# A small store of zeros as ScalarE's first DMA, ahead of the first tile's store, in a channel shuffle

## Chip, cores and metric

The kernel runs on one core of a Trainium2 chip. The metric is device time in microseconds (us), the median of several executions. All timed executions compared here ran in the fast state, at a granted clock of 1.0; runs looked at once have no state of their own ("unknown"), but the same clock. Traces are of one execution each, with times counted from the start of that execution's span.

## The reference

The input is float32, 16 x 64 x 64 x 256. The 256 channels are regarded as 8 groups of 32 and transposed inside each row:

```
x = x.reshape(batch, h, w, groups, channels_per_group)
x = x.transpose(0, 1, 2, 4, 3)
x = x.reshape(batch, h, w, c)
```

There is no arithmetic. 67.11 MB are read and 67.11 MB are written.

## The kernel before

The rows are cut into 22 tiles of 128 partitions. `_SIZES` gives the rows per partition: a 24-row tile moves 128 rows of 24 KB, 3 MB. SyncE loads a tile, VectorE shuffles it in pieces of 8 rows into PSUM, ScalarE copies each piece back to the same buffer, and ScalarE issues the store. So loads and stores go through different queues: in the trace, q1 is SyncE's (loads) and q10 is ScalarE's (stores). There are eight tile buffers, and loads run far ahead. SyncE, VectorE and ScalarE are engines of the core; PSUM is the buffer in which the shuffled pieces stand. A packet is one DMA record of the trace: one row of a tile is one packet, 24 KB for most tiles.

```
_SIZES = [24] * 20 + [8, 24]
_BUFS = 8
_PIECE = 8
# ... set-up cut ...
first = 0
for q in _SIZES:
    buf = pool.tile([P, biggest * c], F32, name="buf")
    nc.sync.dma_start(out=buf[:, : q * c], in_=rows(x_flat, first, q))
    for k in range(0, q, _PIECE):
        piece = buf[:, k * c : (k + _PIECE) * c]
        bounce = psum.tile([P, _PIECE * c], F32, name="bounce")
        nc.vector.tensor_copy(
            out=bounce.rearrange("p (i j g) -> p i j g", j=CPG, g=G),
            in_=piece.rearrange("p (i g j) -> p i j g", g=G, j=CPG),
        )
        nc.scalar.copy(out=piece, in_=bounce)
    nc.scalar.dma_start(out=rows(out_flat, first, q), in_=buf[:, : q * c])
    first += P * q
```

Of the kernel before, what the change touches and what calls it, by code (L numbers as in the profile page):

```python
# [1 line left out]

# [4 lines left out]


F32 = mybir.dt.float32
P = 128  # L10

_SIZES = [24] * 20 + [8, 24]
_BUFS = 8

_PIECE = 8


@with_exitstack
def kernel(
    ctx: ExitStack,  # L20
    tc: tile.TileContext,
    x: bass.AP,
    groups: bass.AP,
    out: bass.AP,
):
    nc = tc.nc
    b, h, w, c = x.shape
    G = int(groups)
    CPG = c // G
    assert G * CPG == c  # L30
    assert sum(_SIZES) * P == b * h * w
    biggest = max(_SIZES)

    x_flat = x.rearrange("b h w c -> (b h w c)")
    out_flat = out.rearrange("b h w c -> (b h w c)")

    pool = ctx.enter_context(tc.tile_pool(name="pool", bufs=_BUFS))
    psum = ctx.enter_context(
        tc.tile_pool(name="psum", bufs=2, space=bass.MemoryType.PSUM)
    )  # L40

    def rows(flat, first, q):

        return flat[first * c : (first + P * q) * c].rearrange("(p f) -> p f", p=P)

    ctx.enter_context(tc.manual_schedule(engines=None))
    first = 0
    for q in _SIZES:
        buf = pool.tile([P, biggest * c], F32, name="buf")
        nc.sync.dma_start(out=buf[:, : q * c], in_=rows(x_flat, first, q))  # L50
        for k in range(0, q, _PIECE):
# [11 lines that stand above are left out]
# [1 line left out]
_INS = ['x', 'groups']  # L64
_OUTS = [((16, 64, 64, 256), 'float32')]

_NUMBERS = {'groups': 8}


# [26 lines left out]
```

## Time and profile before

| what | value |
|---|---|
| time, median of 3 before the prediction | 317.67 us (317.38 to 317.92) |
| span of the profiled execution | 315.9 us |
| bytes moved | 134.24 MB, mean 425 GB/s |
| VectorE busy, ScalarE busy | 72%, 38% |

The page of the kernel before, cut to the rows on which the reading rests. The span is cut into 40 equal slices of 7.9 us; a DMA digit is the busy share in tenths, and GB/s is what the 16 DMA engines moved in that slice.

```profile
span 315.9 us, 289 instructions
...
DVE 227.9 (72%) x64; ACT 120.3 (38%) x65; POOL 0.2 (0%) x4
...
DMA  8999999999999999999999999999999999999997
GB/s 296 439 442 380 436 429 433 433 439 433 423 442 433 426 442 426 426 442 426 433 436 427 433 436 436 433 426 437 433 423 448 423 429 444 429 423 433 439 432 302
```

The DMA engines are busy everywhere; no other engine is. Three slices fall short: the first (the start), the last (the end) and the fourth, with 380 GB/s. The fourth covers 23.7 to 31.6 us. The timeline of ScalarE shows what happens there: ScalarE issues its very first DMA, the store of the first tile. The columns are start, duration, engine, line, operation, and in brackets what the engine waited for.

```profile
11.10 1.28 ACT L58 ACT_TABLE_LOAD   x1 [11.10 <-DMA buf<-in_x_dram]
...
23.68 0.37 ACTq L59 DMA_DIRECT2D out_dram<-buf  x1
...
164.29 0.34 ACTq L59 DMA_DIRECT2D out_dram<-buf  x1
```

The last line is a later store.

To size this, I spread each DMA packet's bytes evenly over the packet's recorded duration, and call "loss" the length of a window less the bytes moved in it divided by 433 GB/s. The figure 433 is the most that any window of 5 us moved in this trace; it also is what 16 packets of 24 KB in every 0.908 us come to, the spacing measured in undisturbed traffic. The trace stays at 432 to 433 GB/s in nearly every 5 us window (53 of 63), so an undisturbed one has a "loss" of 0.00 to 0.01 us. All losses below are such sums over one trace. (The recorded texts took theirs at a slightly higher rate, which no trace shows and which is cut there; their losses are greater by about 0.02 us for each 5 us of a window. For the experiments I converted the sums from that rate, so the last digit can be off by one.)

```
kernel before, window     loss     seen in the packets
  0 to  5 us              2.84 us  first load packet at 1.74 us; first packets take 1.3 to 2.3 us
  5 to 25 us              0.02 us  loads alone, 0.912 us a packet of 24 KB
 25 to 30 us              0.75 us  load packets stretch to 1.2 to 1.9 us; first store packet at 27.69 us
164 to 174 us             0.02 us  stores begin again after a pause of 9.5 us
```

The windows view prints the same dip (columns: window, its length, busy time of VectorE, ScalarE and GpSimd with instruction counts, TensorE clock, DMA share, GB/s). It books all of a packet's bytes at the packet's start, so short windows jump by some per cent; the loss sums do not.

```profile
15.00:25.00 10.00, 10.00 (x3) 5.28 (x3) 0.00 (x0) 1.00 1.00 433
25.00:35.00 10.00, 10.00 (x4) 5.60 (x3) 0.00 (x0) 1.00 1.01 401
35.00:45.00 10.00, 10.00 (x4) 5.59 (x3) 0.00 (x0) 1.00 1.00 433
...
154.00:164.00 10.00, 0.00 (x0) 0.00 (x0) 0.00 (x0) 1.00 1.01 433
164.00:174.00 10.00, 7.38 (x3) 5.50 (x3) 0.00 (x0) 1.00 1.01 433
```

The last two lines are the restart of stores at 164 us, where 0.02 us is lost.

### The profile page before, as it was taken

The numbers are of one execution on the slowest core, as the hardware profiler recorded it, in microseconds if no ns is written. First come the engines' busy times: TensorE is split into PE (matmuls) and PEld (weight loads), VectorE is DVE, ScalarE is ACT, GpSimd is POOL, SyncE is SP. The second block draws the span as 40 slices with busy tenths as digits, with TensorE's granted clock in tenths as the row PEclk, the third lists the DMA queues.
The fourth block names the chain that finished last, engine by engine and source line by source line (L and its number), as shares of the span: only waits on it lengthen the run. The fifth ranks groups of instructions, "written<-read, shape, count | busy, mean of one in ns | idle before, by whom it ended". The sixth has DMA issues, their size and how long they took to land.

```text
span 315.9 us, 289 instructions
## 1 busy us (share of the span) xinstructions
DVE 227.9 (72%) x64; ACT 120.3 (38%) x65; POOL 0.2 (0%) x4
## 2 busy tenths in 40 slices
DVE  0699999959587685957008986999970299999900
ACT  0354455525252424330015416545500444555420
POOL 0000000000000000000000000000000000000000
DMA  8999999999999999999999999999999999999997
GB/s 296 439 442 380 436 429 433 433 439 433 423 442 433 426 442 426 426 442 426 433 436 427 433 436 436 433 426 437 433 423 448 423 429 444 429 423 433 439 432 302
DMA packets 6338, 134.24 MB, mean 425 GB/s; under 512 B 704, under 2 KB 704, under 8 KB 704
## 3 DMA queue, kind: packets, MB, share of 16 engines
q1 hardware_dynamic: 3168, 67.11, 49.9%
q10 hardware_dynamic: 3168, 67.11, 49.4%
q14 instruction: 2, 0.02, 0.0%
HBM read 67.11 MB, written 67.11 MB: 425 GB/s over the span
## 4 chain that ended last, share of the span: by engine, by line
DVE 54%; another core or an unknown queue 23%; issue 8%; ACT 5%; DMA 3%; DVEq 1%; ACTq 0%
DVE bounce L54 54%; ACT buf L58 5%; DMA buf<-in_x_dram 3%; DVEq L91 1%; ACTq L59 0%; DVEq L54 0%; ACTq L58 0%
## 5 line engine op out<-in xcount | busy, mean ns | idle before, releaser
L54 DVE COPY bounce<-buf 128x2048 f32<-128x2048 f32 x64 | 227.9, 3636 | 72.6 <-ACT buf L58 38.8
L58 ACT COPY buf<-bounce 128x2048 f32<-128x2048 f32 x64 | 119.0, 1866 | 171.1 <-DVE bounce L54 115.3
L58 ACT ACT_TABLE_LOAD x1 | 1.3, 1283 | 11.1 <-DMA buf<-in_x_dram 11.1
L77 POOL MEMSET const-bfloat16-1.0<- 128x1 bf16 x1 | 0.1, 102 | 0.0
L77 POOL MEMSET const-uint8-127<- 128x1 uint8 x1 | 0.1, 101 | 0.0
L77 POOL MEMSET const-float32-0.0<- 128x1 f32 x1 | 0.1, 99 | 0.2 <-issue 0.2
L77 POOL MEMSET const-float32-1.0<- 128x1 f32 x1 | 0.1, 98 | 0.0
## 6 DMA issues: line engine op xcount, KB each, us to landing
buf<-in_x_dram SPq DMA_DIRECT2D x21, 3072.0 KB, 58.4
out_dram<-buf ACTq DMA_DIRECT2D x21, 3072.0 KB, 24.2
buf<-in_x_dram SPq DMA_DIRECT2D x1, 1024.0 KB, 46.0
out_dram<-buf ACTq DMA_DIRECT2D x1, 1024.0 KB, 15.8
```

Source lines behind the costliest of these rows:

```text
L54: nc.vector.tensor_copy(out=bounce.rearrange("p (i j g) -> p i j g", j=CPG, g=G), in_=piece.rearrange("p (i g j) -> p i j g", g=G, j=CPG),)
L58: nc.scalar.copy(out=piece, in_=bounce)
L77: nc = _bacc.Bacc("TRN2", target_bir_lowering=False, num_devices=1)
L91: with _tile.TileContext(nc) as tc:
```

## The change

The intent: whatever the first store costs, pay it at the start, where ScalarE and VectorE are idle (until about 11 us) and the loads are slow anyway (296 GB/s in the first slice). A tile of zeros is made, and 512 B of each of the first tile's 128 rows is stored as ScalarE's first DMA. The first tile's real store waits for it and overwrites it, so the result is right.

```diff
+_EARLY = 128
 ...
+    early = ctx.enter_context(tc.tile_pool(name="early", bufs=1))
 ...
+    if _EARLY:
+        zeros = early.tile([P, _EARLY], F32, name="zeros")
+        nc.vector.memset(zeros, 0.0)
+        nc.scalar.dma_start(out=rows(out_flat, 0, _SIZES[0])[:, :_EARLY], in_=zeros)
```

More of the change, by code (lines that the diff above doesn't have):

```diff
@@ L46 @@
     ctx.enter_context(tc.manual_schedule(engines=None))
+    if _EARLY:
+        zeros = early.tile([P, _EARLY], F32, name="zeros")
+        nc.vector.memset(zeros, 0.0)
+        nc.scalar.dma_start(out=rows(out_flat, 0, _SIZES[0])[:, :_EARLY], in_=zeros)
     first = 0
-    for q in _SIZES:
+    for t, q in enumerate(_SIZES):
         buf = pool.tile([P, biggest * c], F32, name="buf")
```

## The prediction

> What bounds the kernel now: the 16 DMA engines. The page's slice row shows DMA at 9 tenths in every slice but the first and last, 134.24 MB at a mean of 425 GB/s over a 315.9 us span; VectorE is busy 72%, ScalarE 38%. [...] its packet records give 432 to 433 GB/s in nearly every 5 us window, for loads, stores or both. So time falls only where the DMA engines lose it. [...] 0 to 5 us loses 2.85 us (the first load packet starts at 1.74 us, and the first packets take 1.5 to 2.3 us against 0.912 us later); 25 to 30 us loses 0.77 us; the end about 2 us; all else 0.03 us per 5 us.
>
> The loss at 25 to 30 us is what the change aims at. ScalarE issues its first store at 23.68 us; from 25.2 us the running load packets stretch from 0.91 to 1.2 to 1.9 us, and the first store packet starts only at 27.69 us. The page shows 380 GB/s in the fourth slice. It is the first use of that queue, not the mixing of loads and stores: at 164.29 us a store is issued to an empty store queue amid full load traffic, its first packet comes 3.5 us later, and the rate stays at 432 GB/s. So a first-use cost of about 0.75 us, once.
>
> What the change adds. A VectorE memset, when VectorE idles until 11.05 us: free. One ScalarE issue (0.34 to 0.37 us in the timeline) near 1 us, where ScalarE idles until 11.10 us: free. 64 KB in 128 rows of 512 B: from the trace's 8 KB packets (0.309 us) and 24 KB packets (0.912 us) I estimate 0.03 us per row, 8 per engine, about 0.2 us of DMA time. The first tile's store waits for this store too, which should land before 8 us: no wait. The extra DMA turns the eight completion semaphores by one: SyncE's sixth load now waits for the first to land (about 11 us), where before the seventh was the first that waited. Five loads of about 7.2 us each are queued, so nothing starves. The later waits (stores held by a load's semaphore, as at 138 to 164 us) keep their pattern.
>
> How much is critical. The engines are full from 30 to 310 us, so what is saved at 27 us moves everything after it. Uncertain is where the first-use cost goes when paid at 1 to 5 us: hidden in the loads' own slow start (gain 0.55 to 0.75 us), or added to it (net loss 0.2 us). Hiding, at least in part, seems likelier.
>
> Predicted time: 317.3 us against 317.67; range 316.6 to 318.1. Faster by over 2%: 0.01; within 2%: 0.98; slower by over 2%: 0.01.
>
> What would show it. Right: the fourth slice rises from 380 to about 430 GB/s; the first tile's store gets its first packet about 3.5 us after issue, with no stretched load packets; the first slice's 296 GB/s falls by no more than 10. Wrong: the fourth slice stays low (the cost is then the first large store's), or the first slice loses what the fourth gains.
>
> What would make it wrong: those two, or the semaphore turn changing when stores are held, so that the last stores, whose issue follows VectorE's chain (last issue 302.46 us, first packet 306.56 us), no longer queue behind one another.

The sum: 317.67 us less 0.55 to 0.75 us if the first-use cost hides in the loads' slow start (316.92 to 317.12), or plus 0.2 us if it is added to it (317.87); the 317.3 lies between, nearer to the first. At 433 GB/s the losses that it lists come to 2.84 us (0 to 5 us), 0.75 us (25 to 30 us), about 1.9 us (the end) and 0.01 us for each other 5 us.

## The result and the profile after

| | median | range | runs |
|---|---|---|---|
| before | 317.63 us | 317.38 to 317.92 | 6 |
| after | 317.83 us | 317.73 to 318.17 | 6 |

The ratio is 1.0007, with a 95% interval of 0.9995 to 1.002: the same time. A ratio here is the mean time of one kernel's fast runs over that of the other's fast runs of the same rounds, so it is not quite the ratio of the medians.

The page of the kernel after, the same rows and the early store's own line (size, and us from issue to landing):

```profile
span 316.0 us, 291 instructions
...
DVE 228.0 (72%) x65; ACT 120.4 (38%) x65; POOL 0.2 (0%) x4
...
DMA  8999999999999999999999999999999999999997
GB/s 299 441 429 386 442 436 429 429 439 429 426 442 439 414 445 436 417 445 432 426 436 434 426 436 436 439 420 440 432 423 442 429 429 442 428 429 429 439 431 302
...
out_dram<-zeros ACTq DMA_DIRECT2D x1, 64.0 KB, 12.0
```

The fourth slice is still low, 386 GB/s. The windows view says the same:

```profile
15.00:25.00 10.00, 10.00 (x3) 5.41 (x3) 0.00 (x0) 1.00 1.00 433
25.00:35.00 10.00, 10.00 (x4) 5.59 (x3) 0.00 (x0) 1.00 0.99 398
35.00:45.00 10.00, 10.00 (x4) 5.50 (x3) 0.00 (x0) 1.00 1.00 433
```

In packet terms, 25 to 30 us loses 0.70 us (0.75 before), and 0 to 5 us loses 2.76 us (2.84 before). Nothing moved from one place to the other. The timeline of the kernel after shows that the new work itself did what it was meant to, early and beside idle engines:

```profile
0.82 0.17 DVE L52 MEMSET zeros<- 128x128 f32 x1 [0.82 <-PEq L85]
1.02 0.41 ACTq L53 DMA_DIRECT2D out_dram<-zeros  x1
11.18 32.02 DVE L62 COPY bounce<-buf 128x2048 f32<-128x2048 f32 x9 [10.19 <-DMA buf<-in_x_dram]
...
23.81 0.34 ACTq L67 DMA_DIRECT2D out_dram<-buf  x1
```

VectorE's first copy comes 0.13 us later than before (11.18 against 11.05) and so does the first tile's store (23.81 against 23.68). That is about what 64 KB of zeros would cost, 0.15 us at 433 GB/s, but it is not shown to be that: traces of five other kernels that begin like the one before have the first copy at 10.66 to 10.94 us. The first real store then meets the old trouble: its first packet comes at 27.65 us, after load packets of up to 1.82 us.

One surprise is the 12.0 us which the 64 KB took to land. The records show where they went: the first 512 B packet (0.027 us each) starts at 5.17 us, 4.15 us after the issue began; the last ends at 11.77 us, 6.6 us later; and the landing is recorded 1.26 us after that. In the 6.6 us, on each engine the eight start about 0.93 us apart, one after each 24 KB load packet of 0.912 us. (The records name no engine; packets are put together by their times.) In this trace, then, the turn changes after every single record: one row of a load stands between any two rows of the small store.

So the time was forecast well and its reason was not: the loss isn't the first use of ScalarE's queue. The experiments ask what it is.

### The profile page after: what moved, and what is told of

It reads as the page before. It is cut to its first block, busy times and chain, and to the rows that moved or that the text cites. A ratio compares the mean times of both kernels' runs of the same rounds, so it can differ in the third digit from the quotient of the medians.

```text
span 316.0 us, 291 instructions
## 1 busy us (share of the span) xinstructions
DVE 228.0 (72%) x65; ACT 120.4 (38%) x65; POOL 0.2 (0%) x4
## 4 chain that ended last, share of the span: by engine, by line
DVE 56%; another core or an unknown queue 22%; issue 9%; ACT 4%; DMA 3%; DVEq 1%; ACTq 0%
DVE bounce L62 56%; ACT buf L66 4%; DMA buf<-in_x_dram 3%; DVEq L99 1%; ACTq L67 0%; DVEq L62 0%; ACTq L66 0%
```

## Experiments

Twelve kernels, each changed for one question (the second drain also re-cuts the tiles); all gave the right result. The theories as they stood:

- Q: the first bulk use of ScalarE's queue, in either direction.
- A (later F): a one-time event at the first bulk write of an execution.
- B: the first tile's store itself, or that moment of the run.
- C: any restart of stores after a long pause.
- S, formed after the first eight runs: a fresh settling of the engines' relative timing, due when bulk stores join loads that have run alone since the engines last stood idle.

### A bulk early store: 1 MB

Edit, against the kernel after:

```diff
-_EARLY = 128
+_EARLY = 2048
```

> The early store of zeros is 1 MB (8 KB rows) in place of 64 KB. It costs about 2.4 us of DMA time [...]. Theory A (the loss of 0.7 us at 25 to 30 us belongs to the first bulk write, whatever issues it): the loss moves into the early store, the 5 us around the first tile's store lose under 0.2 us [...], and the time is about 317.7 + 2.4 = 320.1, less up to 0.7 where it hides in the loads' slow start. Theory B (it belongs to the first tile's store itself or to that moment): the loss of 0.7 us stays there, time about 320.2. Theory C (it comes whenever stores begin again after a pause of over 10 us in full load traffic): stays there too.

Measured: 319.88 us against 317.61 (ratio 1.0073, 1.0058 to 1.0088), so +2.3 us for 1 MB that costs 2.4 us at 433 GB/s. Windows view of this run:

```profile
4.00:14.00 10.00, 1.11 (x1) 1.06 (x1) 0.00 (x0) 1.00 0.98 397
...
25.00:35.00 10.00, 10.00 (x4) 4.94 (x4) 0.00 (x0) 1.00 1.00 433
```

The dip is at the early store now, and it is gone at the first tile's store, which is issued at 25.52 us: 25 to 35 us loses 0.00 us. The window 5 to 25 us loses 0.57 us, 0.55 above the 0.02 of before. So the loss can be moved, and moving it doesn't remove it: 0 to 35 us loses 3.33 us in all, against 3.62 before, a gain of 0.3 us for 2.4 us of bytes. B falls, since the same first tile's store begins at nearly the same moment without a loss.

### All of the first tile's bytes: 3 MB

```diff
-        nc.scalar.dma_start(out=rows(out_flat, 0, _SIZES[0])[:, :_EARLY], in_=zeros)
+        for e in range(0, _SIZES[0] * c, _EARLY):
+            nc.scalar.dma_start(
+                out=rows(out_flat, 0, _SIZES[0])[:, e : e + _EARLY], in_=zeros
+            )
```

with `_EARLY = 2048`.

> Three early stores of 1 MB of zeros, which touch every byte that the first tile's store writes. Costs 7.2 us of DMA time, so about 324.9 us. Theory A: no loss over 0.2 us where the first tile's store begins. If the loss goes here but not with the 1 MB store alone, it belongs to the addresses in HBM, not to the write path. Theories B and C: the loss of 0.7 us stays.

Measured: 324.91 us (ratio 1.0231, 1.0215 to 1.0246). The loss again sits at the early stores (0.56 us from 5 to 30 us), and 30 to 50 us, where real stores begin, loses 0.12 us, some 0.1 above the usual. The 1 MB store already did this while it touched a third of the bytes, so the loss doesn't need every address of the first tile to be written beforehand in order to move.

### ScalarE's queue warmed by a load

ScalarE issues the second tile's load as its first DMA; there are no zeros. Edit against the kernel before:

```diff
+        if t == 0:
+            ahead[1] = pool.tile([P, biggest * c], F32, name="buf")
+            nc.scalar.dma_start(
+                out=ahead[1][:, : q * c], in_=rows(x_flat, first + P * q, q)
+            )
```

and the loop takes `ahead[1]` at its second turn in place of a new tile and load.

> No zeros; the load of the second tile is issued from ScalarE as its first DMA, so the queue has carried 3 MB before its first store and no bytes are added. If the loss belongs to the first bulk use of ScalarE's queue in either direction, it is gone at the first store (under 0.2 us) and the time falls by up to 0.7 us to about 317.0. Theory A (bulk write) and C: the loss of 0.7 us stays at the first store, time 317.5 to 318. The first tile lands later, near 17 us, as both loads share the engines.

Measured: 317.84 us (ratio 1.0006, 0.9989 to 1.0023). The first store is issued at 30.45 us in this run, and the loss goes with it: 0.80 us from 30 to 40 us. Its windows:

```profile
20.00:30.00 10.00, 10.00 (x4) 5.18 (x3) 0.00 (x0) 1.00 1.00 433
30.00:40.00 10.00, 10.00 (x4) 4.94 (x4) 0.00 (x0) 1.00 1.02 406
```

Q falls: the queue had carried 3 MB, and its first store paid all the same.

### Holding stores back: a pause in mid-run

Edit against the kernel before (the second and third run widen the set of tiles):

```diff
+        held.append((rows(out_flat, first, q), buf[:, : q * c]))
+        if t not in (8, 9):
+            for dst, src in held:
+                nc.scalar.dma_start(out=dst, in_=src)
+            held = []
-        nc.scalar.dma_start(out=rows(out_flat, first, q), in_=buf[:, : q * c])
```

> The stores of tiles 8 and 9 are held until the copies of tile 10 are done, so that no store moves for over 20 us in the middle of the run while loads go on, as in the first 27 us. Theory C (a pause in stores brings the loss back): a second loss of about 0.7 us, with load packets stretched to 1.2 to 1.9 us, where tile 8's store starts. Theories A and B: no such loss there, packets stay at 0.91 us; the loss at 25 to 30 us as before.

Measured: no store packet starts from 142.5 to 155.0 us, only 12.5 us, short of the 20 expected. 150 to 160 us loses 0.02 us. One look: 317.43 us. Next, with tiles 8, 9 and 10:

> Stores of tiles 8, 9 and 10 held until tile 11 is copied: the earlier run with two held tiles made a pause of only 12.5 us, this should make one of over 20 us, near the 27 us before the first store. Pause theory: a second loss of about 0.7 us where tile 8's store starts, with packets of 1.2 to 1.9 us. First-bulk-write theory: none, packets stay at 0.91 us. If the loads run dry in the pause, a different loss shows before the restart, with no stretched packets.

Measured: a pause of 23 us (142.6 to 165.6); 160 to 170 us loses 0.01 us. One look: 318.38 us. The longest, with tiles 8 to 11, was run last, after the drains below had raised the question again:

> Stores of tiles 8 to 11 held until tile 12 is copied: a pause of about 33 us in stores, longer than the 27 us at the start and the 28.7 us of the drains, while loads keep the engines busy. Theory S: under 0.1 us lost where stores begin again, packets at 0.91 us, as the relative timing of the engines has not been broken. Length of the pause: 0.3 to 1.0 us lost there with packets of 1.2 to 1.9 us. If the loads run dry before the stores begin again, the run tells nothing on this.

Measured: a pause of 34 us (142.2 to 176.4), longer than the 27 us before the very first store. Loads were still running at the restart. 172 to 182 us loses 0.01 us. One look: 318.16 us. Its windows around the restart:

```profile
160.00:170.00 10.00, 10.00 (x4) 4.94 (x4) 0.00 (x0) 1.00 1.01 435
173.00:183.00 10.00, 6.84 (x2) 2.34 (x2) 0.00 (x0) 1.00 1.00 433
```

C falls as it stands: the length of the pause alone doesn't bring the loss back. But the held tiles kept their buffers, so SyncE's next loads had to wait and few loads were left at the long pauses' ends; this comes up again after the drains.

### How much early store is enough

Three kernels between 64 KB and 1 MB. The first stores 16 rows of 8 KB (`[:16, :_EARLY]` with `_EARLY = 2048`), the second has `_EARLY = 256`, the third `_EARLY = 1024`.

> Early store of 128 KB in 16 rows of 8 KB. If each of the 16 engines takes one row, each moves one long packet instead of eight short ones. The 1 MB early store had taken the loss to itself, the 64 KB one had not. If what counts is one long packet per engine (burst of one engine), the loss of 0.7 us is gone at the first tile's store (under 0.2 us) and shows around the early store. If what counts is the amount moved, it stays at the first tile's store, or most of it. Time 317.7 to 318.1 unless the loss hides in the loads' slow start, then near 317.2.

> The same 128 KB in 128 rows of 1 KB, eight packets an engine. If long packets count: the loss of 0.7 us stays at the first tile's store though the run beside it with the same bytes lost it. If the amount counts: the two runs look alike there. Time about 317.9.

> 512 KB in rows of 4 KB, between 64 KB (loss stays, 0.72 us) and 1 MB (loss gone from the first tile's store). Amount: a loss at the first tile's store in between, 0.1 to 0.5 us. A single event set off by the first long write: gone, under 0.1 us over the usual 0.03, and it shows by the early store instead. Time 318.7 to 319.0 (1.2 us of bytes).

```
early store          packets per engine  loss 5-25 us  loss at first tile's store  time
none (before)        -                   0.02          0.75                        317.61 (7 runs)
64 KB (after)        8 x 512 B           0.06          0.70                        317.83 (6 runs)
128 KB, 16 rows      1 x 8 KB            0.04          0.68 (25 to 32 us)          318.03 (4 runs)
128 KB, 128 rows     8 x 1 KB            0.06          0.95                        318.24 (1 run)
512 KB               8 x 4 KB            0.17          1.01 (25 to 32 us)          319.36 (1 run)
1 MB                 8 x 8 KB            0.57          0.00 (25 to 35 us)          319.88 (4 runs)
```

(The packets per engine are the rows divided by 16; the records name no engine. The window for the first tile's store is 25 to 30 us where none is given. The ratio of the 16-row kernel to the one before is 1.0015, 0.9999 to 1.0032.)

One long packet per engine doesn't do it, nor does 512 KB; 1 MB does. I had expected 512 KB either to split the loss or to remove it from the first tile's store. It did neither: it lost a little early and as much as ever later, a little more than once in all. The time was also above the 318.7 to 319.0 expected. A single event that happens once doesn't fit this well. The amount isn't the only thing that differs between these kernels: the last early packet starts 13.0 us before the first packet of the first tile's store in the 1 MB kernel, and 14.2 us (512 KB) to 20.1 us (128 KB, 16 rows) before it in the others.

### Draining the engines in mid-run

Before loading tiles 8 and 15, SyncE reads back 64 KB of the tile stored last. It must wait for that store, so the DMA engines stand idle (for about 1.4 us in the traces); then loads restart alone, as at the beginning. Edit against the kernel before:

```diff
+        if t in (8, 15):
+            back = seen.tile([P, 128], F32, name="back")
+            nc.sync.dma_start(
+                out=back, in_=rows(out_flat, first - P * q, q)[:, :128]
+            )
```

> Before the loads of tiles 8 and 15, SyncE reads back a 64 KB piece of the tile stored last, so it waits until all stores have landed and the DMA engines stand idle; then loads run alone for some 20 us until the next store, as at the start. Theory F (a one-time cost of the first bulk write in an execution): no loss where stores begin again after either drain, load packets stay at 0.91 us. Theory S (the 16 engines run loads in a fixed relative timing, in which the first bulk store finds them in conflict; they are stretched until they stand in another timing, which then lasts as long as the engines stay busy): after each drain the loads restart with stretched packets and a new timing, and where stores begin again 0.3 to 1.0 us is lost with packets of 1.2 to 1.9 us. The time rises by 30 to 70 us in either case.

Measured: 329.91 us, one look; the rise is only 12 us, not 30 to 70, because stores went on filling most of the time without loads (the standstill was the 1.4 us named above). The first drain's read-back in SyncE's queue, and the windows around where stores begin again after each drain:

```profile
120.74 0.33 SPq L52 DMA_DIRECT2D back<-out_dram  x1
...
132.00:142.00 10.00, 10.00 (x4) 3.73 (x2) 0.00 (x0) 1.00 1.00 433
142.00:152.00 10.00, 10.00 (x4) 5.60 (x3) 0.00 (x0) 1.00 1.02 406
...
238.00:248.00 10.00, 10.00 (x4) 3.89 (x3) 0.00 (x0) 1.00 1.00 431
248.00:258.00 10.00, 10.00 (x3) 5.44 (x3) 0.00 (x0) 1.00 1.01 398
```

The loss comes back both times: 0.76 us from 145 to 150 us and 0.87 us from 250 to 255 us, with load packets of up to 1.80 us, against 0.77 us at this run's first store. A one-time event (A, F) falls. But the pauses in stores were 28.7 us, longer than the 23 us tried so far, so length of the pause was back in play. Two runs separate it: the 34 us pause above, with engines kept busy, and a drain with a short pause. For the latter, the tile before each drain is held and stored after an 8-row tile that is loaded first:

```diff
-_SIZES = [24] * 20 + [8, 24]
+_SIZES = [24] * 8 + [8] + [24] * 6 + [8] + [24] * 5 + [8, 8, 24]
 ...
+        if t not in (7, 14):
+            for dst, src in held:
+                nc.scalar.dma_start(out=dst, in_=src)
+            held = []
```

The drain here reads the tile stored before the held one.

> Both drains again, but the store of the tile before each is held, and a tile of 8 rows is loaded first after it, so that stores begin again some 15 us after the last one ended, less than the pauses of 12.5 and 23 us that cost nothing while the loads ran through. If what brings the loss back is the engines having stood idle and started again with loads alone (theory S): again 0.3 to 1.0 us lost, with packets of over 1.2 us, where stores begin after each drain. If it is the length of the pause in stores (over 25 us, as the 28.7 us of both drains before): under 0.1 us lost there.

Measured: pauses of 14.8 us (111.9 to 126.8) and 15.1 us (208.6 to 223.7). The restarts lose 1.11 us (122 to 129 us) and 1.16 us (219 to 225 us), somewhat above the range expected. One look: 335.96 us. The first of them:

```profile
120.00:130.00 10.00, 5.82 (x3) 1.87 (x1) 0.00 (x0) 1.00 0.98 374
130.00:140.00 10.00, 7.13 (x3) 5.60 (x3) 0.00 (x0) 1.00 1.00 433
```

So 34 us without stores cost 0.01 us while loads kept the engines busy, and 15 us cost over 1 us when the engines stood idle in between. The length of the pause alone is not what counts. That the standstill is what counts is argued, not shown, because the runs with held stores changed a second thing: how many loads were still outstanding when stores began again. The list counts it in tiles of 3 MB, at the issue of the store, as the loads that SyncE had issued less the bytes that its queue had moved; the pause runs from start to start of store packets.

```
stores begin (again)         pause        loads outstanding   loss
before, 164 us                9.5 us      3.9 tiles           0.02 us
tiles 8, 9 held              12.5         3.7                 0.02
1 MB early, first tile       13.0         4.3                 0.00
tiles 8 to 10 held           23           2.2                 0.01
tiles 8 to 11 held           34           0.7                 0.01
512 KB early, first tile     14.2         4.2                 1.01
64 KB early, first tile      15.9         4.1                 0.70
short pause, two drains      14.8, 15.1   4.4, 4.4            1.11, 1.16
two drains                   28.8, 28.7   4.1, 3.5            0.76, 0.87
```

A rival fits every line of it: a pause of more than some 13 to 14 us while several tiles of loads are outstanding. It would also explain why 1 MB early suffices and 512 KB doesn't, which theory S leaves open. No run separates the two: that needs a long pause in stores with a full queue of loads and no standstill. Each drain also brought the standstill, a 64 KB read-back and a restart of loads together.

### The first store, smaller and earlier

```diff
-_SIZES = [24] * 20 + [8, 24]
+_SIZES = [8] + [24] * 21
```

> The tile of 8 rows comes first in place of last but one, so the first store (1 MB, of 8 KB rows) is issued near 10 us and not at 23.7. Both theories: the loss moves with the first bulk store to about 12 to 16 us, 0.3 to 1.0 us, and 25 to 30 us loses nothing. If it stays at 25 to 30 us, it belongs to that moment (SyncE's seventh or eighth load issue) and both fall. Time within 0.6 us of 317.6, no gain as the engines lose as much.

Measured: 317.21 us, one look, beside 317.71 for the kernel before on that chip; with one run each and a range of 317.38 to 318.34 us for the kernel before over all its runs, no gain is shown. The first store (8 KB rows) is issued at 11.21 us, and 12 to 25 us loses 0.60 us. Contrary to what I expected, the next store (24 KB rows, first packet at 29.05 us after a pause of 5.5 us) costs again, though less: 25 to 32 us loses 0.24 us. Neither S nor the rival above says why.

### What the packets show of the engines' timing

All traces show a second thing, read from the start times of the 24 KB packets. In undisturbed traffic 16 packets start in every 0.908 us, one for each of the 16 engines as I read it (the records name no engine), and the 16 starts in one such period form a pattern. Below it is given in ns, after the widest gap, rounded to 10 (a list worked out from the packet records):

```
before, 15 us  loads alone          0 60 140 200 240 390 390 410 490 520 520 590 590 620 620 650
before, 23 us  loads alone          0 60 140 200 240 390 390 410 490 520 520 590 590 620 620 650
before, 33 us  after first store    0 50 140 150 210 240 250 250 330 480 520 540 540 570 650 660
before, 120 us both                 0 50 140 150 210 240 250 250 330 480 520 540 540 570 650 660
before, 161 us loads alone (pause)  0 50 140 150 210 240 250 250 330 480 520 540 550 570 650 660

1 MB early, 25 us  loads alone      0 70 80 80 80 110 120 140 150 220 270 270 300 370 410 610
1 MB early, 33 us  after tile's st. 0 70 80 80 90 110 120 140 150 220 270 270 300 370 410 610

drain, 127 us  loads alone          0 10 30 40 130 130 200 250 270 310 340 340 370 390 520 650
drain, 140 us  loads alone          0 10 30 40 130 130 200 250 270 310 340 340 370 390 520 650
drain, 153 us  after restart        0 0 30 50 70 110 170 190 240 300 320 380 380 520 570 580
```

The pattern stands still for tens of microseconds. It is remade where the loss occurs (before: 23 to 33 us; drain: 140 to 153 us), and it is kept where stores begin without loss (1 MB early: 25 to 33 us). The pattern made at the first store is still there at 161 us, when loads run alone again, and the restart at 164 us costs 0.02 us (one load packet of 1.18 us there, and one of the sixteen starts moves). Theory S rests on this: it takes the loss for the time in which the engines pass into another relative timing. That the pattern and the loss go together is seen; that the one causes the other is my guess, and no run shows it or what would bring it about. One thing is still to be explained by any theory: most of the loss comes before any store packet is on record. Between the issue of the store and its first packet 0.52 us are lost in the kernel before, about 0.6 and 0.7 us at the drains and about 0.9 and 1.0 us at the short ones. What goes on in that time the traces don't show.

## Why the prediction was right, and where it was wrong

- The time. Forecast 317.3, range 316.6 to 318.1; measured 317.83. Inside the range, but on the side of the branch that it called less likely, "added to it (net loss 0.2 us)". The difference of 0.2 us is itself within the interval of the measurement. That the number came out inside the range was luck: the range of 1.5 us held the outcomes of both branches, and the first-use cost that it was built on was not what the kernel paid.
- What bounds the kernel: right. In the experiments added bytes came back as time at the DMA rate: 1 MB cost 2.3 us, 3 MB 7.3 us, against 2.4 and 7.3 at 433 GB/s. The 512 KB, in one run, cost more: 1.75 us against 1.2.
- The costs of the added work: right. The memset took 0.17 us beside an idle VectorE, the issue 0.41 us beside an idle ScalarE, and the first copy came 0.13 us later (estimate 0.2), which is within what traces of like kernels differ by.
- The early store "should land before 8 us": wrong. It landed at about 13 us: its first packet started only at 5.17 us, and its rows took 6.6 us as they alternated with load packets. It still cost no wait, with the first real store issued at 23.81 us.
- The step that failed: "It is the first use of that queue, not the mixing of loads and stores". It rested on one contrast, the free restart at 164 us (0.02 us lost). But at 164 us three things differed from 23.68 us: the queue had been used, the engines had been running without a stop since loads and stores were first mixed, and stores had paused for only 9.5 us. The prediction saw only the first. The load from ScalarE's queue (0.80 us lost at the first store all the same) rules the first out, and the drains (0.76 to 1.16 us lost again at queues long in use) rule out any cost paid once. What they bring back recurs; whether it hangs on the standstill or on a long pause in stores with loads outstanding stays open.
- Hence "Hiding, at least in part, seems likelier" answered a question that did not arise: 64 KB neither paid the cost early nor spared it later. Where more bytes did move it, with 1 MB, the losses up to 35 us fell by 0.3 us only, against 2.4 us for the bytes.
- The signs named in advance worked: "the fourth slice stays low" was listed as the sign of a wrong mechanism, and it stayed at 386. Its gloss, "the cost is then the first large store's", holds for the start of a run, but not as a one-time cost: later stores pay it again after a drain.
- The eight semaphores on which the traces record the landings turned by one place as forecast (SyncE's sixth load was issued at 11.17 us, before at 3.34), and this changed nothing that mattered: the first store was issued 0.13 us later, and the last at 302.38 us against 302.46.

What stays open: whether the standstill or the long pause with loads outstanding brings the loss back; with it, why 1 MB suffices and 512 KB doesn't; why the 8-row first tile pays twice; and what goes on in the time that is lost. Losses of single traces spread (0.6 to 1.0 us at a first store of 24 KB rows in the kernels that begin like the one before), so differences of 0.2 us between them mean little. No version tried beats the kernel before by more than its spread.

## What to carry to other kernels

A warm-up only helps if what it warms is what is cold: before adding one, test it once at a size that must work (here 1 MB), and see whether the dip moves. When a later event is free and the first one is not, list everything that differs between them, not just "first"; forcing the suspected condition again in mid-run (here a drain) tells a one-time cost from one that recurs. And ask what a test changes besides what it is meant to: holding stores back to make a pause also kept buffers full and ran the queue of loads down, so that the longest pauses tell less than they seem to. In these traces each new mix of loads and stores after a standstill of the DMA engines cost about 0.8 to 1.2 us on top of the idle time.
